# Two-layer hybrid block: the low part of a third of the feed-forward weight units from an accumulating load

## The chip, the cores and the metric

The kernel runs on one core of one Trainium2 chip. The metric is the device time of one execution in microseconds (us), the median of several runs of the same program. TensorE is written PE, its weight loads PEld, VectorE is DVE, ScalarE is ACT, GpSimd is POOL, and SP is the engine that issues most of the transfers.

## What is computed

The reference applies two layers to 256 tokens of width 1024, all in float32:

```
for i in range(DEPTH):
    x = x + 0.5 * swiglu(rmsnorm(x, ffn1_norm[i]), ffn1_w1[i], ffn1_w3[i], ffn1_w2[i])
    x = x + hybrid_mixer(rmsnorm(x, mix_norm[i]), w_in[i], ...)
    x = x + 0.5 * swiglu(rmsnorm(x, ffn2_norm[i]), ffn2_w1[i], ffn2_w3[i], ffn2_w2[i])
    gate = jax.nn.sigmoid(rmsnorm(x, ple_norm[i]) @ ple_gate[i])
    x = x + gate * (p[i] @ ple_proj[i])
return rmsnorm(x, final_norm)
```

where `swiglu(h, w1, w3, w2) = (silu(h @ w1) * (h @ w3)) @ w2` with an inner width of 2816. Each of the four feed-forward stages (two a layer) multiplies by 1024 x 5632 and then by 2816 x 1024 weights. The change touches these four stages alone.

## The kernel before

**Products in two parts.** A float32 product is made of three products of 12-bit parts (`mm3`, L280): high by high, high by low, low by high. So each weight tile is needed twice in the core's memory, as `hi` (the value rounded to the type fp32r) and as `lo` (what the rounding left).

**The stream of weights.** All weights come in units of 128 x 2048 numbers (1 MB), in the order of their use, through the class `Stream`. `issue` (L143) loads a unit into one of 3 `raw` buffers (L149, a transfer issued by SP) and splits it by halves of 1024 columns into a `hi` and a `lo` tile, of which there are 5 each:

```
nc.scalar.activation(hi[:, s:f], raw[:, a + s:a + f], AF.Copy)
nc.vector.tensor_tensor(lo[:, s:f], raw[:, a + s:a + f], hi[:, s:f].bitcast(F32), op=OP.subtract)
```

ACT makes `hi` (L158) and DVE makes `lo` (L159). `next` (L163) keeps 3 units ahead of the one that is used. A `hi` or `lo` tile can be written again when PE has read it for the last time, and a `raw` buffer can be loaded again when ACT and DVE have read it.

**The feed-forward stage** (`ffn`, L375). The first matrix is used in 11 chunks of 512 columns, two units (four halves, called h0 to h3 here, two blocks of 128 rows each) a chunk. PE goes through a chunk token tile by token tile (`rows`, L338): first all four halves for token tile 0, then all four for token tile 1. Each token tile takes 24 products of 128 x 512. So the halves of a chunk are set free one after another while token tile 1 goes by, and the halves of the next chunk are made into them just then: four halves are in use and the fifth buffer is the next chunk's h0. After each token tile ACT takes a silu (L387), DVE multiplies (L389), PE transposes the result (L277) and ACT and DVE split it (L395, L396). The second matrix is used in 11 units of 2 x 128 rows (`pairs`, L348), each unit wholly before the next; a unit takes 24 products.

**What sets the order.** A scheduler puts each engine's instructions in a fixed order when the program is built; engines run their queues in that order and wait for one another by semaphores. Semaphores of the loads that SP issues are called DMAHW in the rows of the order, those of transfers that POOL issues DMASW. POOL has no work within the feed-forward stages but the reciprocal root of the rows' squares at their end (L298, L299).

Of the kernel before, what the change touches and what calls it, by code (L numbers as in the profile page):

```python
# [13 lines left out]
AF = mybir.ActivationFunctionType  # L14
OP = mybir.AluOpType
# [16 lines left out]
# columns of the constants  # L32
# [11 lines left out]
# columns of a layer's small weights  # L44
# [53 lines left out]
def lay_out(i):  # L98
    """The arrays of the program: the inputs' own numbers in the order in which the core reads them."""
# [36 lines left out]
class Stream:  # L136
    """The weights' units in the order of their use: load, then split into two parts of 12 bits."""
# [5 lines left out]
    def issue(self, step=HALF_UNIT):  # L143
        ap, cols = self.units[self.issued]
# [6 lines left out]
        for a in range(0, cols, HALF_UNIT):  # L151
# [3 lines left out]
            hi, lo = k.tile("hi", [128, HALF_UNIT], F32R), k.tile("lo", [128, HALF_UNIT], F32R)  # L155
            for s in range(0, e, step):
                f = min(e, s + step)
                nc.scalar.activation(hi[:, s:f], raw[:, a + s:a + f], AF.Copy)  # L158
                nc.vector.tensor_tensor(lo[:, s:f], raw[:, a + s:a + f], hi[:, s:f].bitcast(F32), op=OP.subtract)  # L159
# [10 lines left out]
class Kern:  # L170
    # tiles of a tag, and their bytes of a partition
# [18 lines left out]
    # ---- tiles  # L190
# [33 lines left out]
    def constants(self):  # L224
        """What the mixers alone need."""
# [18 lines left out]
    def units(self, stages):  # L244
        a = self.a
        units = []
        for s in stages:
            if s[0] == "ffn":
                _, l, n = s
                units += [(a[f"up{n}"][l, u], UNIT) for u in range(2 * NCH)]  # L250
                units += [(a[f"dn{n}"][l, u], UNIT) for u in range(NCH)]
# [12 lines left out]
        return units  # L264

    # ---- shared pieces
    def took(self, out, passes):
        """Adds about what a product takes, in us: two of 64 rows run side by side."""
        self.pe += max(64, int(np.prod(out.shape[1:]))) * passes / (2400.0 if out.shape[0] > 64 else 4800.0)

    def mm(self, out, lhsT, rhs, start=True, stop=True, part=False):
        """lhsT^T rhs; with part, a bank holds several sums and the first product alone starts it."""
# [12 lines left out]
    def rms(self, t, h, pin=False):  # L285
        """1 / rms of the rows of x, by halves of the columns."""
# [15 lines left out]
    def parts(self, tags, n):  # L302
        """Tiles for the two parts of a feature-major activation of n k-tiles, and the getter of a k-tile's parts."""
# [3 lines left out]
    def advance(self, t, h, rms=True):  # L307
        """What the next stage needs of half the columns of a token tile of x: their transpose times the gain, in two
        parts, and 1 / rms of the rows."""
# [28 lines left out]
    def rows(self, xT, cols, tmajor, bs, kt=4):  # L338
        """x @ w for a chunk of w's columns held in units of kt k-tiles: a bank for each of the token tiles."""
# [8 lines left out]
    def pairs(self, xT, nu, tail, ready=None):  # L348
        """x @ w for w held in units of 2 k-tiles x 1024 columns; the last units are taken token tile by token tile."""
# [24 lines left out]
    # ---- stages  # L374
# [68 lines left out]
    def scaled(self, t, h):  # L443
        """1 / rms of the rows, and after the second half the output."""
# [12 lines left out]
    # ---- the mixer  # L457
    def weave(self, *streams):
        """Emits the streams' steps in about the order in which the tensor engine can take them. The first streams go
        first; a step yields how long, in us, its results take to come, or False while it waits for another stream."""  # L460
# [120 lines left out]
    def gates(self, o, z0):  # L581
        """Sigmoids of the gates and of beta, and what the decays come to."""
# [35 lines left out]
    def rope(self, z, t, nh):  # L618
        """Rotary embedding of z [128, nh, 64], the rows of a token tile."""
# [9 lines left out]
    def compress(self, g, z0, cw1):  # L629
        """The compressed keys [(kv, d), kv, n] in two parts, the compressed values [(i, kv, n), (i, kv), d] in blocks."""  # L630
# [61 lines left out]
    def silu2(self, y):  # L692
        """2 silu(y) in place of y [128, 512]."""
# [4 lines left out]
    def conv(self, g, name, z, f0):  # L698
        """z^T of 4 heads after the short convolution and twice its silu."""
# [22 lines left out]
    def products(self, name, g, t):  # L722
        """A bank with the products of a token tile's keys [j] with its keys or queries [i]."""
# [6 lines left out]
    def gdn_rows(self, g, name, t):  # L730
        """A bank with the rows of a token tile of feature-major heads."""
# [5 lines left out]
    def squares(self, ss, src):  # L737
        """Sums of the squares of [128, 4, 128] by head."""
# [350 lines left out]
```

## Time and profile before

| | |
|---|---|
| median of 3 runs | 1197.44 us (1197.08 to 1198.85) |
| profiled execution, first to last instruction (span) | 1193.4 us |
| median over that span | 4.0 us |
| PE busy | 1167.4 us (98%) |
| DVE busy | 738.0 us (62%) |
| ACT busy | 643.4 us (54%) |
| POOL busy | 98.2 us (8%) |
| transfers | 194.15 MB, mean 163 GB/s |

The profile gives the span of the profiled execution and no time of its own beside it; the runs' times are 3.7 to 5.5 us above that span, which lies ahead of the first and behind the last instruction. Busy time is the sum of an engine's instructions. A busy PE can still wait inside a stretch for as long as a matmul's recorded end covers it, so the start-to-start distance of its products is the better measure. Idle time of an engine that is not the bottleneck costs nothing.

### The profile page before, as it was taken

To read this page: it belongs to the slowest core of one execution; us is meant where nothing else is said; L and a number is where in the kernel's file an instruction comes from. 1 tells how busy PE (TensorE), PEld (TensorE's weight loads), DVE (VectorE), ACT (ScalarE), POOL (GpSimd) and SP (SyncE) were. 2 spreads that over 40 slices of the span, in tenths; PEclk is the share of its full clock that TensorE was granted. 3 is DMA by queue.
4 is the path that set the end of the run, shared out by engine and by line. 5 is a ranking of instruction groups with operands and counts; after the bars stand their busy time and mean duration, and the time that the engine had idled before them with its cause. 6 is when DMAs were issued, how large, how long until landed. Compare 5 with 4: busy or idle time off the path is not lost.

```text
span 1193.4 us, 16045 instructions
## 1 busy us (share of the span) xinstructions
PE 1167.4 (98%) x6222; PEld 934.7 (78%) x6222; DVE 738.0 (62%) x1191; ACT 643.4 (54%) x1157; POOL 98.2 (8%) x137
## 2 busy tenths in 40 slices
PE   8999999989999999999999999999899999999996
PEld 6888888877677788888878888887676778888885
DVE  5655546887846655645665564469777465565454
ACT  7544536645666554534665454375367565454463
POOL 0000000270101000000000000004500100000011
PEclk9999999999999999999999999999999999999998
DMA  8546653431213545464464575543221244555640
GB/s 314 189 164 221 237 199 125 179 108 66 86 57 141 194 163 208 171 213 154 177 212 158 195 259 199 179 178 111 102 72 71 72 164 162 203 183 201 207 176 36
DMA packets 29292, 194.15 MB, mean 163 GB/s; under 512 B 3232, under 2 KB 3616, under 8 KB 7200
## 3 DMA queue, kind: packets, MB, share of 16 engines
q1 hardware_dynamic: 28496, 191.56, 45.0%
q10 hardware_dynamic: 720, 1.57, 0.4%
q8 instruction: 49, 0.80, 0.3%
q14 instruction: 27, 0.22, 0.1%
HBM read 192.07 MB, written 1.05 MB: 162 GB/s over the span
## 4 chain that ended last, share of the span: by engine, by line
PE 91%; DVE 4%; issue 2%; ACT 1%; POOL 1%; DMA 1%; POOLq 0%; SPq 0%; ACTq 0%
PE bA L273 49%; PE bN L273 32%; PE bG L273 4%; PE bG L277 4%; PE bN L277 1%; DVE lo L159 1%; ACT hi L158 1%; DMA raw<-win 1%; POOL mn L625 0%; DMA x<-x 0%; ACT junk L925 0%; DVE y L714 0%; DVE mn L626 0%; DVE ad L786 0%; DVE g L450 0%
## 5 line engine op out<-in xcount | busy, mean ns | idle before, releaser
L273 PE MATMUL bA<-hi,xT 128*128 128x512 f32 (+1 forms) x1856 | 605.2, 398 | 1.1 <-DVE xT L327 0.5
L159 DVE TENSOR_TENSOR lo<-raw,hi 128x1024 fp32r<-128x1024 f32 (+2 forms) x358 | 437.0, 1225 | 225.2 <-ACT hi L158 204.0
L158 ACT ACTIVATE hi<-raw 128x1024 fp32r<-128x1024 f32 (+2 forms) x358 | 373.0, 1047 | 228.5 <-PE bN L273 115.8
L273 PEld LDWEIGHTS bA<-hi,xT 128*128 128x128 f32 x1856 | 345.4, 189 | 76.3 <-issue 5.9
L273 PE MATMUL bA<-lo,xT 128*128 128x512 f32 (+1 forms) x928 | 361.1, 391 | 0.0
L273 PEld LDWEIGHTS bA<-lo,xT 128*128 128x128 f32 x928 | 175.3, 189 | 32.9 <-issue 0.7
L273 PE MATMUL bN<-hi,n 128*128 128x512 f32 x480 | 155.2, 394 | 0.0
L273 PE MATMUL bN<-hi,g 128*128 128x512 f32 x448 | 139.9, 391 | 0.0
L273 PEld LDWEIGHTS bN<-hi,n 128*128 128x128 f32 x480 | 90.4, 188 | 18.4 <-issue 0.7
L273 PEld LDWEIGHTS bN<-hi,g 128*128 128x128 f32 x448 | 83.8, 188 | 17.2
L273 PE MATMUL bN<-lo,n 128*128 128x512 f32 x240 | 95.3, 397 | 0.0
L389 DVE SCALAR_TENSOR_TENSOR m<-bA,r,m 128x256 f32<-128x256 f32 x88 | 42.2, 479 | 79.7 <-ACT m L387 79.7
L273 PE MATMUL bN<-lo,g 128*128 128x512 f32 x224 | 87.8, 392 | 0.0
L387 ACT ACTIVATE m<-bA,r 128x256 f32<-128x256 f32 x88 | 41.3, 470 | 72.9 <-PE bA L273 69.7
L298 POOL TENSOR_SCALAR r<-ss 128x1 f32<-128x1 f32 x18 | 5.9, 330 | 823.0 <-ACT junk L291 823.0
L273 PEld LDWEIGHTS bN<-lo,n 128*128 128x128 f32 x240 | 45.1, 188 | 9.6 <-issue 1.1
L273 PEld LDWEIGHTS bN<-lo,g 128*128 128x128 f32 x224 | 42.1, 188 | 8.5
L327 DVE SCALAR_TENSOR_TENSOR xT<-bG,first,xT 128x128 fp32r<-128x128 f32 x96 | 31.7, 346 | 25.2 <-ACT xT L326 25.1
L326 ACT ACTIVATE xT<-bG,first 128x128 fp32r<-128x128 f32 x96 | 32.8, 361 | 16.1 <-DVE xT L327 16.0
L395 ACT ACTIVATE g<-bG 128x256 fp32r<-128x256 f32 x48 | 18.0, 374 | 42.3 <-PE bG L277 42.2
L277 PE MATMUL bG<-first,m 128*128 128x128 f32 x192 | 36.9, 273 | 2.7 <-DVE m L931 2.5
L277 PEld LDWEIGHTS bG<-first,m 128*128 128x128 f32 x192 | 25.8, 140 | 17.3 <-issue 4.5
(218 smaller groups left out, 967.8 us busy)
## 6 DMA issues: line engine op xcount, KB each, us to landing
raw<-up SPq DMA_DIRECT2D x86, 1024.0 KB, 4.9
raw<-dn SPq DMA_DIRECT2D x44, 1024.0 KB, 5.0
raw<-win SPq DMA_DIRECT2D x24, 1024.0 KB, 4.8
raw<-wout SPq DMA_DIRECT2D x8, 1024.0 KB, 4.9
raw<-gate SPq DMA_DIRECT2D x8, 1024.0 KB, 4.9
cw<-cw SPq DMA_DIRECT2D x8, 512.0 KB, 8.0
raw<-up SPq DMA_DIRECT2D x4, 512.0 KB, 7.1
raw<-proj SPq DMA_DIRECT2D x2, 1024.0 KB, 4.8
```

The source lines that it names most:

```text
L158: nc.scalar.activation(hi[:, s:f], raw[:, a + s:a + f], AF.Copy)
L159: nc.vector.tensor_tensor(lo[:, s:f], raw[:, a + s:a + f], hi[:, s:f].bitcast(F32), op=OP.subtract)
L273: self.nc.tensor.matmul(out, lhsT, rhs, start=start, stop=stop, skip_group_check=part)
L277: self.nc.tensor.transpose(out, x, self.ident[:n, :n])
L298: nc.gpsimd.tensor_scalar(r, self.ss[:, 0:1], self.ss[:, 1:2], EPS, op0=OP.add, op1=OP.add)
L326: nc.scalar.activation(hi[h][:, i, cs], b[:, i, :], AF.Copy, scale=g)
L327: nc.vector.scalar_tensor_tensor(lo[h][:, i, cs], b[:, i, :], g, hi[h][:, i, cs].bitcast(F32), op0=OP.mult, op1=OP.subtract)
L387: nc.scalar.activation(s, bs[t][:, :256], AF.Silu, scale=r[t])
L389: nc.vector.scalar_tensor_tensor(h, bs[t][:, 256:], r[t], s, op0=OP.mult, op1=OP.mult)
L395: nc.scalar.activation(hh[c // 2][o], b, AF.Copy)
```

## The change

In every feed-forward stage the units 3, 7, 11, 15 and 19 of the first matrix (the second unit, h2 and h3, of the chunks 1, 3, 5, 7 and 9) and the units 1, 3, 5, 7 and 9 of the second are marked `summed`: 10 of 33. For a half of such a unit ACT writes the negative of the rounded weights into `lo`, then `hi` as before, and POOL issues a transfer that reads the same half of the unit from the chip's memory a second time and adds it to what stands in `lo`. VectorE's subtraction of that half is gone. Units of the other stages are not summed. The lines of the changed kernel are 7 further down; the diff also takes out comments, which is left out here.

```diff
-        ap, cols = self.units[self.issued]
+        ap, cols, summed = self.units[self.issued]
...
             hi, lo = k.tile("hi", [128, HALF_UNIT], F32R), k.tile("lo", [128, HALF_UNIT], F32R)
+            if summed:
+                nc.scalar.activation(lo[:, :e], raw[:, a:a + e], AF.Copy, scale=-1.0)
+                nc.scalar.activation(hi[:, :e], raw[:, a:a + e], AF.Copy)
+                nc.gpsimd.dma_start(lo[:, :e], ap[:, a:a + e], accum_op=OP.add)
+                parts.append((hi, lo))
+                continue
             for s in range(0, e, step):
...
-                units += [(a[f"up{n}"][l, u], UNIT) for u in range(2 * NCH)]
-                units += [(a[f"dn{n}"][l, u], UNIT) for u in range(NCH)]
+                units += [(a[f"up{n}"][l, u], UNIT, u % 4 == 3) for u in range(2 * NCH)]
+                units += [(a[f"dn{n}"][l, u], UNIT, u % 2 == 1) for u in range(NCH)]
...
-        return units
+        return [u if len(u) > 2 else u + (False,) for u in units]
```

How the instructions now stand, at three places. ACT's queue before, in the first feed-forward stage, from h1 of chunk 3 to the silu of chunk 2 (`hi_316` is h1, `hi_390` and `hi_394` are h2 and h3, `hi_400` is the next chunk's h0):

```order
L158 ACTIVATE hi_316<-raw_310 128x1024 [waits PE_49]
L158 ACTIVATE hi_390<-raw_388 128x1024 [waits DMAHW6_49,PE_49]
L158 ACTIVATE hi_394<-raw_388 128x1024 [waits PE_49]
L158 ACTIVATE hi_400<-raw_398 128x1024 [waits DMAHW7_49,PE_49]
L395 ACTIVATE g_177<-bG_462 128x2x128 [waits PE_49]
```

The same place of ACT's queue now (h1 is `hi_318`, h2 is `lo_393` and `hi_392`, h3 is `lo_398` and `hi_397`, the next h0 is `hi_404`):

```order
L165 ACTIVATE hi_318<-raw_312 128x1024 [waits PE_49]
L158 ACTIVATE lo_393<-raw_390 128x1024 [waits DMAHW6_49,PE_49]
L159 ACTIVATE hi_392<-raw_390 128x1024 [waits PE_49]
L158 ACTIVATE lo_398<-raw_390 128x1024 [waits PE_49]
L159 ACTIVATE hi_397<-raw_390 128x1024 [waits PE_49]
L165 ACTIVATE hi_404<-raw_402 128x1024 [waits DMAHW7_49,PE_49]
L402 ACTIVATE g_177<-bG_466 128x2x128 [waits PE_49]
```

Two activations have come in, and h3, the next chunk's h0 and the copy of the transposed result stand behind them.

PE's queue before, where chunk 3 comes to h2 and h3 for token tile 0 (`lo_391` and `lo_395` are their low parts):

```order
L273 MATMUL bA_496<-hi_390,xT_74 128x512 [waits Activation_49]
L273 MATMUL bA_496<-lo_391,xT_74 128x512 [waits DVE_49]
L277 MATMUL bG_471<-first_64,m2_469 128x128 [waits DVE_49]
L277 MATMUL bG_471<-first_64,m2_469 128x128
L273 MATMUL bA_496<-hi_390,xT_76 128x512
L273 MATMUL bA_496<-hi_390,xT_74 128x512
L273 MATMUL bA_496<-lo_391,xT_74 128x512
L273 MATMUL bA_496<-hi_390,xT_76 128x512
L273 MATMUL bA_496<-hi_394,xT_74 128x512 [waits Activation_49]
```

And now:

```order
L280 MATMUL bA_500<-hi_392,xT_74 128x512 [waits Activation_49]
L280 MATMUL bA_500<-lo_393,xT_74 128x512 [waits DMASW2_49]
L280 MATMUL bA_500<-hi_392,xT_76 128x512
L280 MATMUL bA_500<-hi_392,xT_74 128x512
L280 MATMUL bA_500<-lo_393,xT_74 128x512
L280 MATMUL bA_500<-hi_392,xT_76 128x512
L284 MATMUL bG_475<-first_64,m2_473 128x128 [waits DVE_49]
L284 MATMUL bG_475<-first_64,m2_473 128x128
L280 MATMUL bA_500<-hi_397,xT_74 128x512 [waits Activation_49]
L280 MATMUL bA_500<-lo_398,xT_74 128x512 [waits DMASW3_49]
```

The first product with the low part of h2 and of h3 now waits for a transfer that POOL issued, and the two transposes stand four products later.

POOL's queue now, in the first feed-forward stage from h2 of chunk 3 on; before, none of these transfers was there:

```order
L160 DMA lo_393<-up1 128x1024 [waits DVE_49,Activation_49]
L160 DMA lo_398<-up1 128x1024 [waits DVE_49,Activation_49]
L160 DMA lo_571<-up1 128x1024 [waits DMASW1_49,DVE_49,Activation_49]
L160 DMA lo_576<-up1 128x1024 [waits DVE_49,Activation_49]
L160 DMA lo_749<-up1 128x1024 [waits DMASW3_49,DVE_49,Activation_49]
```

There are 80 such transfers of 512 KB in the program, 20 a feed-forward stage, and each waits for the activation that wrote the negative part.

## Rows read from the trace of the kernel before

**Rows 1.** The page, busy us (share of the span) by engine.
```profile
PE 1167.4 (98%) x6222; PEld 934.7 (78%) x6222; DVE 738.0 (62%) x1191; ACT 643.4 (54%) x1157; POOL 98.2 (8%) x137
```

**Rows 2.** Stretches of 30 us; the last three columns: PE clock, transfer share, GB/s.
```profile
core 0: us, PE busy (x) PEld busy (x) DVE busy (x) ACT busy (x) POOL busy (x), PEclk, DMA share, GB/s
90.00:120.00 30.00, 30.00 (x138) 24.51 (x137) 16.91 (x23) 14.18 (x22) 0.00 (x0) 1.00 0.60 220
...
240.00:270.00 30.00, 26.83 (x285) 21.34 (x285) 26.61 (x44) 12.38 (x19) 21.80 (x22) 0.94 0.31 111
```

**Rows 3.** Chain of waits, chunk 7 of the first feed-forward stage: start, us, what.
```profile
90.64 3.24 PE bA L273 x14
93.88 0.22 PE bG L277 x2
94.09 7.78 PE bA L273 x34
101.87 0.22 PE bG L277 x2
```

**Rows 4.** Groups by line: count, busy us, mean ns, idle before by releaser.
```profile
L159 DVE TENSOR_TENSOR lo<-raw,hi 128x1024 fp32r<-128x1024 f32 (+2 forms) x358 | 437.0, 1225 | 225.2 <-ACT hi L158 204.0
L158 ACT ACTIVATE hi<-raw 128x1024 fp32r<-128x1024 f32 (+2 forms) x358 | 373.0, 1047 | 228.5 <-PE bN L273 115.8 <-PE bA L273 109.9 <-DMA raw<-win 1.8
```

**Rows 5.** Timeline of ACT, chunk 6 to 7: start us, us, instruction, idle before.
```profile
86.37 1.06 ACT L158 ACTIVATE hi<-raw 128x1024 fp32r<-128x1024 f32 x1 [0.89 <-PE bA L273]
87.73 1.06 ACT L158 ACTIVATE hi<-raw 128x1024 fp32r<-128x1024 f32 x1 [0.30 <-PE bA L273]
89.09 1.06 ACT L158 ACTIVATE hi<-raw 128x1024 fp32r<-128x1024 f32 x1 [0.30 <-PE bA L273]
90.45 1.06 ACT L158 ACTIVATE hi<-raw 128x1024 fp32r<-128x1024 f32 x1 [0.30 <-PE bA L273]
...
91.68 0.47 ACT L387 ACTIVATE m<-bA,r 128x256 f32<-128x256 f32 x1
```

**Rows 6.** Timeline of PE, chunk 7: first low products of h2 and h3.
```profile
93.48 0.39 PE L273 MATMUL bA<-lo,xT 128*128 128x512 f32 x1
...
95.11 0.39 PE L273 MATMUL bA<-lo,xT 128*128 128x512 f32 x1
```

**Rows 7.** DMA issues: kind, count, KB each, median us from issue to landing.
```profile
raw<-up SPq DMA_DIRECT2D x86, 1024.0 KB, 4.9
...
raw<-win SPq DMA_DIRECT2D x4, 432.0 KB, 3.2
```

**Rows 8.** Timeline of SP's queue: the two loads beside chunk 7's start, merged.
```profile
88.72 3.05 SPq L149 DMA_DIRECT2D raw<-up  x2
```

**Rows 9.** One stretch over both loads' data; columns as in rows 2.
```profile
89.00:96.00 7.00, 7.00 (x34) 5.70 (x33) 4.65 (x6) 3.14 (x5) 0.00 (x0) 1.00 0.84 300
```

**Rows 10.** Timeline of DVE, chunk 7: the multiplication that its transposes wait for.
```profile
93.02 0.47 DVE L389 SCALAR_TENSOR_TENSOR m<-bA,r,m 128x256 f32<-128x256 f32 x1
```

**Rows 11.** Timeline of ACT, second matrix: second half of unit 3.
```profile
146.22 1.06 ACT L158 ACTIVATE hi<-raw 128x1024 fp32r<-128x1024 f32 x1 [3.02 <-PE bN L273]
```

**Rows 12.** Timeline of PE, second matrix: its first low products, unit 3, both halves.
```profile
153.04 0.39 PE L273 MATMUL bN<-lo,g 128*128 128x512 f32 x1
...
154.41 0.39 PE L273 MATMUL bN<-lo,g 128*128 128x512 f32 x1
```

**Rows 13.** Stretches of 1 us around a pause of PE in the mixer; columns as in rows 2.
```profile
250.00:251.00 1.00, 0.00 (x0) 0.00 (x0) 0.97 (x4) 0.97 (x1) 0.74 (x2) 1.00 0.00 0
251.00:252.00 1.00, 0.00 (x0) 0.00 (x0) 1.00 (x5) 0.09 (x1) 0.62 (x2) 1.00 0.00 0
...
253.00:254.00 1.00, 1.00 (x16) 0.89 (x12) 1.00 (x2) 0.92 (x3) 1.00 (x1) 0.89 0.06 16
254.00:255.00 1.00, 1.00 (x6) 0.35 (x7) 1.00 (x1) 0.72 (x2) 1.00 (x2) 0.50 0.00 0
...
257.00:258.00 1.00, 1.00 (x5) 0.81 (x5) 1.00 (x2) 0.00 (x0) 1.00 (x2) 0.91 0.85 360
```

## Prediction, made before the changed kernel ran

> **What bounds the kernel now.** I read the page's busy times first: PE is busy for 98% of the span, DVE for 62%, ACT for 54%, POOL for 8% [rows 1]. An average hides stages, so the stretches come next: within a feed-forward stage PE is busy 30.00 of 30 us at full clock while the transfer engines are used for 0.60 and POOL for nothing; PE's gaps lie in the mixers (26.83 of 30) [rows 2]. The chain of waits says the same more sharply: chunk 7 of the first stage is nothing but PE's products, 14, then two transposes, then 34, then two transposes, from 90.64 to 102.09, that is 11.45 us [rows 3]. DVE and ACT wait for PE there: `lo` sat idle mostly for `hi`, and `hi` for PE's release of a buffer [rows 4]. So what DVE does is not on the path, and whatever makes a `lo` tile late is.
>
> How late it may be is read from three timelines. ACT makes h1, h2 and h3 of chunk 7 at 86.37, 87.73 and 89.09, each 0.30 us after PE let go of a buffer [rows 5]. PE first multiplies by the low part of h2 at 93.48 and of h3 at 95.11 [rows 6].
>
> **The change, part by part.** *Removed:* 4 stages x 10 units x 2 halves = 80 subtractions on DVE, 80 x 1.225 = 98 us [rows 4]. They lie beside PE's products, so they are worth 0, and with PE's waits in the stages near nothing there is nothing else for them to give back.
>
> *Added on ACT:* 80 activations x 1.047 = 84 us [rows 4]. With h1 from 86.37 and each activation 1.06 us [rows 5], the negative of h2 runs from 87.50 to 88.56, its `hi` to about 89.5, the negative of h3 to 90.5, its `hi` to 91.5, the next chunk's h0 to 92.5 instead of 91.51. The silu behind them, which ended at 92.15 [rows 5], ends near 93.2, and DVE's split of that h0 ends near 93.8, with a copy and the multiplication of 0.47 us behind it; so the multiplication, which started at 93.02 [rows 10], ends near 94.7. The transposes that need it now stand behind 18 products, not 14, so near 94.8: cost 0. If that cover is gone, PE waits there for some tenths.
>
> *Moved on SP:* the loads that wait for a `raw` buffer were issued at 88.72 and about 91.4, where the merged row ends at 91.77 [rows 8]. The first still waits for DVE's h1; the second now waits for ACT's `hi` of h3, about 91.5. No change.
>
> *Added on POOL:* 80 issues. POOL has 0.00 us of other work in the stage [rows 2], so none queues behind another engine's work; the root for the next stage stands behind the last of them and is needed only when those products are over.
>
> *Added transfers, 512 KB each.* This is the term that decides. The low part of h3 can be issued when its negative is written, at 90.5, and is needed at 95.1: it may take 4.6 us; h2's, from 88.6 to 93.5, 4.9. The trace has no accumulating transfer, so I bound its price. Loads of 432 and 1024 KB land 3.2 and 4.9 us after issue [rows 7]: 1.7 us for 592 KB is 2.94 us for 1 MB, and 2.0 us fixed. The two loads of 1 MB beside this place keep the engines busy 0.84 x 7 = 5.9 us, again 2.94 each [rows 9]. So a plain copy of 512 KB costs the engines 1.47 us. An accumulation also has to fetch what stands in `lo`; I take 1.47 us as the lower and twice that, 2.94 us, as the upper price.
>
> The transfers meet exactly those two loads: the first starts at 88.72, the first accumulation at 88.6. *Lower end:* the engines serve POOL's transfers ahead, at a plain copy's price: h3 lands at 90.5 + 2.0 + 1.47 = 94.0, 1.1 us early, PE waits 0. *With the two queues served in turn*, the loads get as much as the accumulations, so h3 lands at 88.7 + 2.0 + 4 x the price: 96.6 at 1.47, 1.5 us late; 102.5 at 2.94, 7.4 us late. *Upper end:* 7.4 us. No row is nearer to one end, so I take the middle, 3.7 us; that is also what turns at one and a half copies (2.2 us) give: 99.5, 4.4 late, less a little for queues that overlap less than assumed. PE cannot win such a wait back, since it is busy in all of the rest. There are 5 such chunks in each of 4 stages: 20 x 3.7 = 74 us.
>
> The Trainium skill, "Collectives: The Full Stack", section "The bandwidth ceiling: the fold count and why AG ≠ RS ≠ AR", says that a transfer that adds runs at about half a copy's rate, because it reads two sources. It speaks against this change; by it the price is 2.94 us and the sum that of my upper end, 20 x 7.4 = 148 us. No row here can show it yet.
>
> *Second matrix.* There the fifth buffer and units used one at a time give more room. The negative of unit 3's second half is written from about 146.2 to 147.3 [rows 11] and needed at 154.41 [rows 12]: 7.1 us; the first half has more. At 2.0 + 2.94, and one load of 2.94 in turn, it takes 7.9 at most, 0.8 late; at the lower price 4.9. I take 0 and keep 0 to 16 us (20 x 0.8) for the range.
>
> *Sum:* 74 us. It is made against the profiled execution, span 1193.4 us, which ends near 1267; the median of the runs is 4.0 us above that span, so I forecast 1197.4 + 74 = **1271 us**.
>
> **The rivals.** *The transfer is hidden anyway (not slower).* If the loads get out of the way, h3 lands at 94.0 as worked out above, and nothing waits: 1197 us. It decides at a time to landing of 4.6 us. For it: the engines are used for only 0.60 of the stage [rows 2]; against it: they are used for 0.84 in just the 7 us that matter [rows 9]. The Trainium skill, "DMA: Bandwidth & Descriptors", section "Anatomy of one DMA — SWDGE (gpsimd) path", fits 2.0 us plus the bytes at 436 GB/s for a transfer from POOL, an estimate of 3.2 us for 512 KB, which sides with this rival; [rows 7] agree on the 2.0 us, on another queue.
>
> *The transfer engines become the bound.* At the double price, two units of the second matrix (2 x 24 products, about 11.0 us by the 34 products in 7.78 us of [rows 3]) need 2 x 2.94 for loads and 2 x 2.94 for accumulations, 11.8 us. Then the first matrix loses 148 us and the second some 20 x 0.8 = 16: 1197 + 164 = 1361 us. For it: an addition in place is more work than a copy; against it: nothing in the trace yet.
>
> *The clock falls.* In the mixer PE did nothing from 250 to 252, and from 253 to 258 the granted clock was 0.89, then 0.50 (1.2 instead of 2.4 GHz), then 0.91 [rows 13]; about 3.4 us at half speed, 1.7 us lost. If each of the 20 waits, at 3.7 us longer than that pause of some 2 us, did the same, 20 x 1.7 = 34 us more: 1305 us. Against it: the wait falls into two, at h2 and at h3, with products between, and dense ones right after, where the pause in the mixer was followed by small products.
>
> *Faster.* DVE's freed 98 us would have to shorten a wait of PE, and the stages have none [rows 2]; only in the passages into the mixers could a microsecond come back.
>
> That the change does not do what it says is excluded by the order: PE's products wait for POOL's transfers.
>
> **How the numbers follow.** The forecast case, PE waiting 1 to 6 us in each of the 20 chunks, gets 0.50 (its own range 1217 to 1317); hidden 0.17; engines as the bound 0.17; the clock 0.13; faster 0.03. The range 1197 to 1340 takes in the hidden case at its low end, the forecast and the clock's 1305, and leaves out the engines' 1361 and what is faster, 0.20 together. A difference under 0.2% (2.4 us) cannot be told from no change here: faster 0.03; same 0.14, most of the hidden case; slower the rest, 0.83.
>
> **What would show it.** Right: DVE's `lo` at 278 instructions and about 340 us busy, ACT about 727 us; in PE's waits a new releaser, POOL's transfer of `lo`, some 20 to 40 times, 1 to 4 us each, in the first matrix alone, at the first low products of h2 and h3; the issues listed with 5 to 9 us to landing. Wrong: no such wait (hidden); waits in the second matrix as well and transfers in use without a gap (engines as the bound); granted clock of 0.50 behind the waits (clock); or PE waiting for ACT or DVE in the chunks that have a summed unit, which would be a mistake in what I costed at 0.

## The result, and the profile after

The change makes the kernel slower by almost a fifth, and by more than the forecast's range allowed.

| | before | after |
|---|---|---|
| median of the runs | 1197.61 us (4 runs) | 1421.09 us (4 runs) |
| ratio | | 1.1881, 95% interval 1.1856 to 1.1906 |
| span of the profiled execution | 1193.4 us | 1419.2 us |
| mean granted clock of PE | 0.994 | 0.942 |

The page of the kernel after: busy time by engine (answers to [rows 1]), three groups (to [rows 4]), the two queues with their packets, MB and share of 16 engines' time, and the issues with count, size and median us to landing (to [rows 7]).

```profile
PE 1239.6 (87%) x6222; PEld 968.6 (68%) x6222; DVE 641.0 (45%) x1111; ACT 712.2 (50%) x1237; POOL 168.0 (12%) x217
...
q1 hardware_dynamic: 28496, 191.56, 38.2%
q0 software_dynamic: 11520, 41.95, 15.9%
...
L166 DVE TENSOR_TENSOR lo<-raw,hi 128x1024 fp32r<-128x1024 f32 (+2 forms) x278 | 339.2, 1225 | 378.5 <-ACT hi L165 370.3
L280 PE MATMUL bA<-lo,xT 128*128 128x512 f32 (+1 forms) x928 | 383.1, 413 | 108.4 <-DMA lo<-up 108.4
...
L158 ACT ACTIVATE lo<-raw 128x1024 fp32r<-128x1024 f32 x80 | 84.5, 1056 | 72.9 <-PE bN L280 70.2
...
raw<-up SPq DMA_DIRECT2D x86, 1024.0 KB, 5.1
raw<-dn SPq DMA_DIRECT2D x44, 1024.0 KB, 7.6
...
lo<-up POOLq DMA_DIRECT2D x40, 512.0 KB, 10.3
lo<-dn POOLq DMA_DIRECT2D x40, 512.0 KB, 8.9
```

PE has the same 6222 products, but it is idle for 1419.2 - 1239.6 = 179.6 us where it was idle for 26.0, and its products take 72.2 us more, at a lower clock. These two, 153.6 and 72.2, are the 225.8 us by which the span grew. A new releaser stands behind the idle time. The accumulations land 10.3 and 8.9 us after their issue, where SP's loads of double the size beside them land after 5.1 and 7.6. What they cost the transfer engines is read from the queues: 15.9% of 1419.2 us for 80 transfers is 2.82 us each, and 38.2% for 191.56 MB is 1.48 us per 512 KB (0.524 MB) of load. An addition costs nearly two such loads, 1.9.

The waits of PE, after (us in total, times, longest):

```profile
PE bA L280 <- DMA lo<-up: 108.4, 39, 5.9
PE bN L280 <- DMA lo<-dn: 42.4, 24, 4.0
```

So 150.8 of the 153.6 us are waits for the low parts: 5.4 us in each of the 20 summed chunks of the first matrix, 2.1 us in each of the 20 summed units of the second.

One chunk shows how it comes about. It is chunk 7 of the first stage again (answers to [rows 3, 5, 6]). ACT's timeline, with h1, then the negative and `hi` of h2, and those of h3:

```profile
112.91 1.06 ACT L165 ACTIVATE hi<-raw 128x1024 fp32r<-128x1024 f32 x1 [0.89 <-PE bA L280]
114.04 1.06 ACT L158 ACTIVATE lo<-raw 128x1024 fp32r<-128x1024 f32 x1
115.01 1.04 ACT L159 ACTIVATE hi<-raw 128x1024 fp32r<-128x1024 f32 x1
115.96 1.04 ACT L158 ACTIVATE lo<-raw 128x1024 fp32r<-128x1024 f32 x1
```

POOL's timeline, the accumulations of h2 of chunk 5, of h2 and h3 of chunk 7, and of h2 of chunk 9:

```profile
83.68 0.86 POOL L160 DMA_DIRECT2D lo<-up  x1 [27.01 <-DVE lo L166]
...
115.40 0.86 POOL L160 DMA_DIRECT2D lo<-up  x1 [28.96 <-DVE lo L166]
117.29 0.86 POOL L160 DMA_DIRECT2D lo<-up  x1 [1.03 <-ACT lo L158]
...
145.10 0.86 POOL L160 DMA_DIRECT2D lo<-up  x1 [26.94 <-DVE lo L166]
```

SP's queue, the two loads beside them (answers to [rows 8]):

```profile
115.26 3.04 SPq L150 DMA_DIRECT2D raw<-up  x2
```

The transfer queues in three stretches, 115.4 to 119.8, 119.8 to 121.8 and 121.8 to 127.9 (packets, MB, share of the engines); q0 carries the accumulations, q1 the loads:

```profile
q1 hardware_dynamic: 125, 1.02, 80.9%
...
q0 software_dynamic: 90, 0.37, 96.9%
q1 hardware_dynamic: 22, 0.05, 6.4%
...
q0 software_dynamic: 197, 0.68, 56.7%
q1 hardware_dynamic: 141, 1.02, 41.8%
```

PE's timeline, the last products before h2's low part, and the first low products of h2 and of h3:

```profile
119.57 0.61 PE L280 MATMUL bA<-hi,xT 128*128 128x512 f32 x2
124.40 0.64 PE L280 MATMUL bA<-lo,xT 128*128 128x512 f32 x1 [4.22 <-DMA lo<-up]
...
128.37 0.49 PE L280 MATMUL bA<-lo,xT 128*128 128x512 f32 x1 [0.77 <-DMA lo<-up]
```

SP's load was issued at 115.26, 0.14 us ahead of h2's accumulation, and the engines moved nearly all of it (1.02 MB) before the first packet of q0, 4.4 us after POOL's issue. Then h2 went nearly alone, and then h3 and the second load shared the engines. Two loads and two accumulations kept them busy until 127.9. At full clock PE would have wanted h2's low part at 120.0 and h3's 1.63 us later [rows 6], at 121.65; it got them at 124.40 and 128.37, so h3's is 6.7 us late.

Stretches, after (columns as in [rows 2]): one of 30 us, then some of 1 us in chunk 7 and in chunk 5, whose first low product of h3 started at 96.90.

```profile
90.00:120.00 30.00, 26.45 (x104) 20.92 (x104) 9.75 (x12) 13.14 (x18) 1.72 (x2) 0.83 0.52 164
...
125.00:126.00 1.00, 1.00 (x4) 0.81 (x3) 0.00 (x0) 0.00 (x0) 0.00 (x0) 0.50 1.00 303
128.00:129.00 1.00, 0.63 (x3) 0.54 (x4) 0.05 (x1) 0.00 (x0) 0.00 (x0) 0.99 0.00 0
...
97.00:98.00 1.00, 1.00 (x3) 0.81 (x4) 0.00 (x0) 0.00 (x0) 0.00 (x0) 0.50 0.00 0
100.00:101.00 1.00, 1.00 (x4) 0.80 (x3) 0.43 (x1) 0.00 (x0) 0.00 (x0) 0.64 0.00 0
```

After the wait for h2 the granted clock is 0.50 (1.2 GHz). In chunk 7 it is back when h3 lands, so the slow products of h2 only filled time in which PE would have waited for h3. In chunk 5 it stays low until about 100.7 (0.64 is the mean from 100 to 101), 3.8 us beyond h3's first low product, which costs 1.9 us. The distances of POOL's issues say the same: 31.7 us from chunk 5 to 7 and 29.7 from 7 to 9, where two chunks took 22.9 before [rows 3].

### The profile page after: what moved, and what is told of

Read it like the earlier page. It is cut to its first block, busy times and chain, and to the rows that moved or that the text cites. A ratio compares the mean times of both kernels' runs of the same rounds, so it can differ in the third digit from the quotient of the medians.

```text
span 1419.2 us, 16263 instructions
## 1 busy us (share of the span) xinstructions
PE 1239.6 (87%) x6222; PEld 968.6 (68%) x6222; DVE 641.0 (45%) x1111; ACT 712.2 (50%) x1237; POOL 168.0 (12%) x217
## 3 DMA queue, kind: packets, MB, share of 16 engines
q1 hardware_dynamic: 28496, 191.56, 38.2%
q0 software_dynamic: 11520, 41.95, 15.9%
## 5 line engine op out<-in xcount | busy, mean ns | idle before, releaser
L280 PE MATMUL bA<-hi,xT 128*128 128x512 f32 (+1 forms) x1856 | 637.8, 415 | 1.3 <-DVE xT L334 0.5
L166 DVE TENSOR_TENSOR lo<-raw,hi 128x1024 fp32r<-128x1024 f32 (+2 forms) x278 | 339.2, 1225 | 378.5 <-ACT hi L165 370.3
L280 PE MATMUL bA<-lo,xT 128*128 128x512 f32 (+1 forms) x928 | 383.1, 413 | 108.4 <-DMA lo<-up 108.4
L280 PEld LDWEIGHTS bA<-hi,xT 128*128 128x128 f32 x1856 | 365.5, 199 | 80.7 <-issue 5.9
L165 ACT ACTIVATE hi<-raw 128x1024 fp32r<-128x1024 f32 (+2 forms) x278 | 287.4, 1040 | 160.4 <-PE bA L280 93.9
L158 ACT ACTIVATE lo<-raw 128x1024 fp32r<-128x1024 f32 x80 | 84.5, 1056 | 72.9 <-PE bN L280 70.2
L160 POOL DMA_DIRECT2D lo<-up x40 | 35.0, 875 | 491.2 <-DVE lo L166 451.1
L396 DVE SCALAR_TENSOR_TENSOR m<-bA,r,m 128x256 f32<-128x256 f32 x88 | 42.1, 479 | 98.1 <-ACT m L394 98.1
L159 ACT ACTIVATE hi<-raw 128x1024 fp32r<-128x1024 f32 x80 | 83.4, 1043 | 0.0
L402 ACT ACTIVATE g<-bG 128x256 fp32r<-128x256 f32 x48 | 18.0, 376 | 121.8 <-PE bG L284 121.8
L160 POOL DMA_DIRECT2D lo<-dn x40 | 34.6, 865 | 315.6 <-ACT lo L158 230.6
L403 DVE TENSOR_TENSOR g<-bG,g 128x256 fp32r<-128x256 f32 x48 | 20.2, 421 | 103.7 <-ACT g L402 103.7
## 6 DMA issues: line engine op xcount, KB each, us to landing
lo<-up POOLq DMA_DIRECT2D x40, 512.0 KB, 10.3
```

The costliest lines, as they stand in the source:

```text
L158: nc.scalar.activation(lo[:, :e], raw[:, a:a + e], AF.Copy, scale=-1.0)
L159: nc.scalar.activation(hi[:, :e], raw[:, a:a + e], AF.Copy)
L160: nc.gpsimd.dma_start(lo[:, :e], ap[:, a:a + e], accum_op=OP.add)
L280: self.nc.tensor.matmul(out, lhsT, rhs, start=start, stop=stop, skip_group_check=part)
L396: nc.vector.scalar_tensor_tensor(h, bs[t][:, 256:], r[t], s, op0=OP.mult, op1=OP.mult)
L402: nc.scalar.activation(hh[c // 2][o], b, AF.Copy)
```

## The experiments

All kernels are built from the changed one. The time of the kernel before, run beside them on the same chip, was 1195.9 to 1196.7 us; losses are against that.

**Which part loses how much.** Only one of the two matrices is summed:

```diff
-                units += [(a[f"dn{n}"][l, u], UNIT, u % 2 == 1) for u in range(NCH)]
+                units += [(a[f"dn{n}"][l, u], UNIT, False) for u in range(NCH)]
```

> Only units of the first matrix are summed (40 transfers); the second matrix is as before the change. Theory A (each late transfer costs its own wait and the half clock behind it, and the two matrices don't touch each other): the 108 us of waits stay, with about 50 to 60 us of slower clock, 1345 to 1370 us, and this kernel's gain over the time before plus that of the other half alone add up to the whole 224 us. Theory B (the two disturb each other, by the clock or the transfers of one stage running into the next): the two parts alone come to less than 180 us together.

and, with the same edit on the line of `up` instead:

> Only units of the second matrix are summed (40 transfers); the first matrix is as before the change. The prediction's step, 0 us here with 0 to 16 us as its range, would give 1197 to 1213 us. Theory A (20 waits of 2.1 us at the second matrix, and a slower clock behind them): 42 us and 10 to 25 us, so 1245 to 1265 us.

The first gave 1359.4 us (ratio 1.1371, 1.1352 to 1.1389), the second 1261.5 us (1.0544, 1.0522 to 1.0567). The losses, 163.3 and 65.4 us, add up to 228.7 where both together cost 223.5, so the parts hardly touch each other. The second matrix, put at 0 in the prediction, loses 65 us. Its waits, in the run that sums it alone:

```profile
PE bN L280 <- DMA lo<-dn: 45.1, 23, 4.2
```

**ACT's work by itself.** VectorE overwrites the negative; there is no transfer:

```diff
-                nc.gpsimd.dma_start(lo[:, :e], ap[:, a:a + e], accum_op=OP.add)
+                nc.vector.tensor_tensor(lo[:, :e], raw[:, a:a + e], hi[:, :e].bitcast(F32), op=OP.subtract)
```

> ACT writes the negative into lo as in the changed kernel, 80 activations more, but no transfer adds to it: VectorE then overwrites it with the difference as before the change. The result is the same. It tests what the 84 us of ACT's work cost by themselves. Theory A (the prediction's step: they lie beside PE's products, cost 0): 1194 to 1200 us. Theory B (ACT's queue makes the copies of the transposed result or the next chunk's first half late): 1 us or more in each of 20 chunks, 1215 us or more.

1198.4 us, ratio 1.0026 (1.0015 to 1.0036), with ACT at 711.5 us. The 80 activations cost 2 to 4 us in all; 2.0 of them are two waits of PE for a multiplication (`PE bG L284 <- DVE m L396`), which the kernel before doesn't have. The rest of the loss is the transfers'.

**Adding or copying.** The same transfers without the addition:

```diff
-                nc.gpsimd.dma_start(lo[:, :e], ap[:, a:a + e], accum_op=OP.add)
+                nc.gpsimd.dma_start(lo[:, :e], ap[:, a:a + e])
```

> The 80 transfers of POOL copy the unit's half into lo instead of adding it to what stands there; everything else, the waits too, is as in the changed kernel. The low part is then the whole weight, so the computed numbers differ. Theory A (the adding itself is dear: twice the engine time of a copy, and a landing 9 to 10 us after issue): without it the queue's engine time falls from 2.82 to about 1.41 us a transfer, the landing to 5 to 6 us, PE's waits for lo in the first matrix from 108 us to 10 to 40 us, and the time from 1421 to between 1200 and 1260 us. Theory B (POOL's way of issuing is slow whatever the transfer does): landing stays at 9 to 10 us and the time at 1400 to 1421 us.

1299.8 us (ratio 1.0866, 1.085 to 1.0883): between the theories. From its page:

```profile
q0 software_dynamic: 11520, 41.95, 10.2%
...
lo<-up POOLq DMA_DIRECT2D x40, 512.0 KB, 7.1
lo<-dn POOLq DMA_DIRECT2D x40, 512.0 KB, 7.2
```

A copy costs the engines 10.2% of 1297.8 us / 80 = 1.65 us in place of 2.82, and the addition is worth 121 us. But a copy too is late, in the first matrix by 3.5 us at h3's first low product (mean of the 20 chunks): 104 us are lost without any addition.

**Earlier transfers.** Halves with a longer lead are summed: h0 of every chunk and the first half of the odd units of the second matrix; then the same without the first two chunks of a stage.

```diff
-            if summed:
+            if summed and a == 0:
...
-                units += [(a[f"up{n}"][l, u], UNIT, u % 4 == 3) for u in range(2 * NCH)]
+                units += [(a[f"up{n}"][l, u], UNIT, u % 2 == 0) for u in range(2 * NCH)]
```

> Halves with more time to come are summed instead: the first half (h0) of every chunk of the first matrix and the first half of units 1, 3, 5, 7 and 9 of the second, 64 transfers in all in place of 80; POOL adds as in the changed kernel. h0 has some 10 us between the writing of its negative and its use, the second matrix' first half about as much. Theory A (only what lands after its use costs): with a landing of 9 to 10 us waits of 0 to 1 us each, 1197 to 1240 us. Theory B (the extra traffic, ACT's extra work or the issuing costs by itself, or slows PE's clock without a wait): 64/80 of the loss or so, over 1300 us.

> As the run that sums the first halves, but without those of the first two chunks of each stage, where the lead is shortest at the start of a stage; 56 transfers, each with some 10 us between the negative and its use. Theory A (an accumulation that lands in time costs nothing, its traffic included): only the second matrix' first halves still wait now and then, some 5 us in all, 1198 to 1208 us. Theory B (the traffic or POOL's and ACT's work cost by themselves): 56/64 of that run's 18 us, 1212 us.

1213.9 us (1.0162, 1.0141 to 1.0183) with 64 transfers and 1203.7 us (1.0065, 1.005 to 1.008) with 56. A stretch of the second run inside the first matrix, and its waits for low parts:

```profile
60.00:120.00 60.00, 60.00 (x275) 48.60 (x274) 28.43 (x38) 34.57 (x49) 4.62 (x6) 1.00 0.80 236
```

```profile
PE bN L280 <- DMA lo<-dn: 4.7, 4, 1.3
PE bA L280 <- DMA lo<-up: 0.6, 1, 0.6
```

The engines are used for 0.80 there, more than in the changed kernel, and PE never stops. These transfers land 8.2 us after their issue and are wanted after 10.6. So neither the traffic nor POOL's issuing costs by itself, as far as 56 transfers show; what costs is landing after the use.

**One transfer a chunk.** Only h3 is summed (`if summed and a > 0`, second matrix not summed).

> Only the last half (h3) of each summed chunk of the first matrix is summed, 20 transfers; h2 and the second matrix are as before the change. Theory A (the transfers of h2 and h3 stand in one queue, and h3 pays for h2's): with half as many bytes in the queue h3 lands some 7 us after its issue, which is 1 us earlier than before as ACT has one activation fewer ahead of it, so PE waits 1 to 2 us in a chunk: 20 to 40 us, 0 to 20 us for the clock, 1220 to 1255 us. Theory B (each transfer costs the same on its own): half of what summing both costs, 163 / 2, or 1278 us.

1339.7 us (1.1202, 1.1165 to 1.1238), a miss for both theories: half the transfers, and 144 of the 163 us remain. They land 9.5 us after issue. h2's accumulation was not what h3 waited for; with it gone, the loads took its place on the engines.

**The loads beside them.** First those of the feed-forward units that aren't summed are left out, with additions and with copies:

> The changed kernel without the loads of the feed-forward units that aren't summed: these split the unit that was loaded last once more, so their numbers are wrong. The 80 accumulations have then next to no other transfers beside them. Theory A (they land late because the loads take turns with them on the transfer engines): landing falls to 5 to 6 us, waits in the first matrix from 108 us to under 40, time 1200 to 1270 us. Theory B (POOL's adding transfer takes 9 us by itself): landing 8 to 10 us, waits near 100 us, time over 1370 us.

> As the run without the loads of the feed-forward units that aren't summed, and with copies in place of additions too; the numbers are wrong for both reasons. By the prediction's rows (2.0 us fixed and 1.47 us of engine time) a copy of 512 KB from POOL that meets nothing lands 3.5 us after its issue, and no wait for lo is left: within 1195 to 1205 us. If instead the start of POOL's transfers takes longer than that of SP's, landing is 5 us or more and some waits stay.

1340.6 us (1.1199, 1.1179 to 1.1219) and 1259.2 us (one run). In the first, theory A missed, and theory B met the landing (9.1 us in the first matrix) but not the time, with waits of 83.3 us there. The copies landed after 6.4 us with 39.6 us of waits, as the last sentence of their expectation has it. The trace shows why: the load of the next summed unit was still issued together with each pair of accumulations, and 1 MB of it went ahead of them. A first packet 4.4 us after the issue could thus be that load or a slow start of POOL's path. A transfer of a quarter of the bytes seemed to speak for the slow start (ACT's line for the negative is cut to 256 columns too):

```diff
-                nc.gpsimd.dma_start(lo[:, :e], ap[:, a:a + e], accum_op=OP.add)
+                nc.gpsimd.dma_start(lo[:, :256], ap[:, a:a + 256], accum_op=OP.add)
+                nc.vector.tensor_tensor(lo[:, 256:e], raw[:, a + 256:a + e], hi[:, 256:e].bitcast(F32),
+                                        op=OP.subtract)
```

> The same 80 halves, but the transfer adds only 256 of the 1024 columns, and VectorE subtracts the other 768 as before the change; ACT writes the negative of those 256 alone. The bytes of a transfer are a quarter (128 KB), its start is the same. Theory A (most of the 9 to 10 us is the start of POOL's transfer, some 4.4 us from issue to the first packet, and its end): landing still 5 to 7 us, waits of some 0 to 1.5 us in a chunk, 1205 to 1250 us. Theory B (a start of 2.0 us as for the loads that SP issues, the rest is bytes): landing near 3 us, no wait, within 1195 to 1203 us.

1239.7 us (1.0362, 1.0345 to 1.0379), and 128 KB still take 6.8 us to land. The number met theory A; its reason was wrong, as the next two runs show, in which no load is left beside the transfers:

> The changed kernel without any load of a feed-forward unit but the first of each stage, those of the summed units included: all split the tile that was loaded last, so the numbers are wrong. In the run that left out the unsummed units' loads, one load of 1 MB was still issued with each pair of accumulations, and the engines served it first. Theory A (that load is what puts the first packet 4.4 us behind the issue): now it comes 1.2 to 1.7 us behind, as where no load was ahead in the changed kernel; landing 5 to 6.5 us, h3 some 1 to 2 us late, 1215 to 1245 us. Theory B (POOL's path starts slowly in the first matrix whatever the loads do): landing 8 to 9 us and some 1340 us as in that run.

> The same, with copies in place of additions; the numbers are wrong for both reasons. Theory A: landing 3.5 to 4.2 us, no wait for lo, 1194 to 1202 us. Theory B: landing 6 us, 1259 us as with one load left.

1246.5 us (1.0413, 1.0393 to 1.0434), just above theory A's range, and 1220.6 us (1.0201, 1.0186 to 1.0217). In the first, POOL issues an accumulation at 75.33 (its timeline, first fence). The queues have no packet from then to 76.8; the second fence is their row from 76.9 to 80.3, and the third the page's issues:

```profile
75.33 0.85 POOL L164 DMA_DIRECT2D lo<-up  x1 [21.99 <-DVE lo L170]
```

```profile
q0 software_dynamic: 140, 0.54, 99.2%
```

```profile
lo<-up POOLq DMA_DIRECT2D x40, 512.0 KB, 5.8
lo<-dn POOLq DMA_DIRECT2D x40, 512.0 KB, 5.7
```

POOL's path starts within about 1.6 us. The other 2.8 us of the 4.4 are the load ahead. But ahead doesn't have to mean issued first. In the run with a quarter of the bytes POOL's issue came 0.50 us before the load's, and the first packet of q0 still only after 3.2 us, with 0.39 MB of the load moved before it (third line, 97.3 to 100.5):

```profile
97.31 0.86 POOL L160 DMA_DIRECT2D lo<-up  x1 [23.32 <-ACT lo L158]
...
97.81 0.33 SPq L150 DMA_DIRECT2D raw<-up  x1
...
q1 hardware_dynamic: 47, 0.39, 55.0%
```

The copies land after 4.6 us in the first matrix; that theory A put them at 3.5 to 4.2 us, without a wait, missed by little in landing and by 19 us in time. Of the 24 us that this run loses, 9.3 are waits for low parts and 4.2 one wait for a multiplication in the first stage. Together (time in us; median landing in the first matrix):

| loads beside the transfers | adding | copying |
|---|---|---|
| all | 1421 (10.3) | 1300 (7.1) |
| one of 1 MB with each pair | 1341 (9.1) | 1259 (6.4) |
| none | 1246 (5.8) | 1221 (4.6) |

**Nothing left out: the loads wait.** The loads are made to come after the accumulations, in the kernel that sums the first matrix alone. POOL reads a column of the raw tile that the next load overwrites, once a low part has landed. With one load held, behind h2:

```diff
+        if summed:
+            held = k.tiny(1, "held")
+            nc.gpsimd.tensor_tensor(held, self.raw[:, :1], parts[0][1][:, :1].bitcast(F32), op=OP.add)
+        self.raw = raw
```

> As the run that sums the first matrix alone (1359 us), with one tiny instruction more a chunk: POOL reads one column of the raw tile of the unit ahead of the summed one together with one column of h2's low part, once that has landed. So SP's load into that raw buffer, which was issued some 0.1 us ahead of h2's accumulation, now waits until h2's low part is there. Nothing is left out. Theory A (the load that is served first makes the accumulations late): landing 5 to 8 us, waits of 1 to 2.5 us a chunk in place of 5.4, 1225 to 1275 us, if the load that now starts some 6 us later doesn't make the next chunk wait. Theory B (the start of POOL's path): within 1% of 1359 us.

1345.4 us (1.1253, 1.1234 to 1.1272), far above theory A's range and at the very edge of theory B's, 1% below 1359. By the time alone B would stand; the waits say otherwise. PE's timeline, the first low products of h2 and h3 of chunk 5:

```profile
87.00 0.50 PE L284 MATMUL bA<-lo,xT 128*128 128x512 f32 x1 [0.70 <-DMA lo<-up]
...
92.48 0.79 PE L284 MATMUL bA<-lo,xT 128*128 128x512 f32 x1 [3.59 <-DMA lo<-up]
```

Against the same chunk with no load held, the wait for h2 went from 4.1 to 0.7 us, and the one for h3 from 1.6 to 3.6: the other load, which the scheduler now put ahead in SP's queue, took turns with h3 instead. So both were held, behind h3 (`parts[1][1]`), by a second read of the unit's own raw tile:

```diff
+            nc.gpsimd.tensor_tensor(held, raw[:, :1], held, op=OP.add)
```

> As the run that sums the first matrix alone (1359 us), but now both loads that come free beside a summed chunk wait: POOL reads a column of the raw tiles of the two units together with one of h3's low part, once that has landed. In the run before, with one load held, the other went ahead of it and took turns with h3, and the waits moved from h2 (4.2 to 0.7 us) to h3 (1.0 to 3.6 us). Nothing is left out. Theory A (a load beside the accumulations makes them late): landing 5.5 to 6 us as in the run without loads, waits of 1.5 to 2 us a chunk, full clock, 1225 to 1250 us, if the two loads, which start some 5 us later, don't make the next chunk wait. Theory B (POOL's path as such, or the addition as such): over 1300 us.

1252.6 us (1.0475, 1.0458 to 1.0493), from 1359.4, just above theory A's range, with the clock at 0.995. Its waits, and ACT in the chunk behind chunk 7:

```profile
PE bA L285 <- DMA lo<-up: 32.5, 39, 2.0
PE bG L289 <- DVE m L401: 10.9, 17, 1.2
...
113.06 2.01 ACT L165 ACTIVATE hi<-raw 128x1024 fp32r<-128x1024 f32 x2 [1.23 <-DMA raw<-up]
```

At least two thirds of the first matrix' loss are the two loads. What is left is 56 us. Some 42 of them lie in the summed chunks, where h3's first low product is still 2.0 us late: the addition's own time against a lead of under 5 us. Some 16 lie in the chunks behind them and are the price of holding the loads: ACT waits for a held load there, and the multiplication that stands behind it makes PE wait, 17 times 0.6 us. No version here is faster than the kernel before.

**The clock.** Products that nobody reads fill PE's waits, then half as many:

```diff
+            if t == 0 and flags[k // kt] and k in (4, 6):
+                self.fill("N", 18 if k == 4 else 12, xT(0, t)[0], us[0](0, cols)[0])
...
+            if (t, h, k % 2) == (0, 0, 1) and flags[k // 2]:
+                self.fill("G", 9, xT(0, t)[0], u(0, 512)[0])
```

> The changed kernel with products that nobody reads put where PE waits: 18 ahead of the first products of h2 and 12 ahead of those of h3 in each summed chunk, 9 ahead of the second half of each summed unit of the second matrix; 780 products of about 0.22 us, some 170 us of work that is thrown away, in a bank that is free. Of the loss of 226 us of span, 72 us are PE's products at a slower clock. Theory A (PE's pauses make the clock fall): with the pauses filled the clock stays at 0.98 or more, the products' 72 us come back for the most part, while what the fillers take beyond the waits (170 less 151) costs up to some 20 us: 1355 to 1390 us. Theory B (the clock falls for another reason, the transfers' or ACT's activity): clock still near 0.94, and the time is 1421 us or more.

> As the run with fillers, with half as many: 9 ahead of h2's products, 6 ahead of h3's, 4 in the second matrix; 380 products in place of 780, some 87 us of work that is thrown away. Theory A (the transfers' landing sets the time, and the slow clock costs only what comes after the last landing of a chunk): waits of 50 to 90 us come back in place of the fillers, the time stays within 10 us of that run's 1412. Theory B (the full number of fillers was longer than the waits, and hid a gain of the full clock): the time falls to 1350 to 1390 us with the clock still over 0.97.

1412.5 us (1.1806, 1.1782 to 1.1831) at a mean clock of 0.991, and 1410.4 us (1.1782, 1.1759 to 1.1806) at 0.967. PE's waits in the first and in the second:

```profile
PE bN L282 <- DMA lo<-dn: 13.7, 9, 2.2
PE bA L282 <- DMA lo<-up: 9.8, 18, 2.6
```

```profile
PE bA L282 <- DMA lo<-up: 51.6, 24, 4.5
PE bN L282 <- DMA lo<-dn: 27.8, 17, 3.3
```

Filling the waits restores the clock, so the waits are what lowers it. But three kernels with clocks of 0.942, 0.967 and 0.991 end within 11 us of each other: the landing sets the time, and PE's speed while it would wait anyway does not. The first expectation (1355 to 1390) missed by taking all of the 72 us of slower products for a loss.

What the clock does cost can be read from the starts of the low products in the three traces, against the same starts in the kernel before. The first column sums the delay, over the 20 summed chunks, from the last low product of h1 to the first of h3, and, over the 20 summed units, from the last low product of the unit before to the first of the second half. The second column sums what is lost behind that, where PE waits for no transfer any more, up to the last low product of the chunk, or of the next unit:

| us, first + second matrix | up to the last late half | behind it |
|---|---|---|
| changed kernel | 140.4 + 47.4 | 22.9 + 13.3 |
| filled | 154.5 + 58.2 | -0.8 + 2.3 |
| half filled | 151.2 + 51.1 | 1.5 + 11.1 |

So the slow clock costs 36 us, half of the 72, and the fillers do give them back. They cost 25 us themselves, since the late halves' products start later by that much; whether that is only the rest of a filler when the transfer lands isn't separated here.

The Trainium skill, "TensorE: Matmul & The Clock Gate", section "HAM oscillation — how this bites in real kernels", counts as the cost of a lowered clock the time spent at it times one half. By the mean clocks (0.058 and 0.006 below full, at half speed twice as long) that is 0.058 x 1419 - 0.006 x 1193 = 75 us here. It is the 72 us of PE's rows, and twice the 36 us by which the kernel is longer for it.

## Why the prediction was right and wrong

*The bound and the direction* were right: PE had nothing to wait for, and whatever made a `lo` tile late was paid in full.

*Removed from DVE:* 97.0 us (738.0 to 641.0) against 98 forecast, worth nothing, as said.

*Added on ACT, at 0:* 2 to 4 us. The busy time came to 712.2 us, not 727, since activations that follow directly start 0.95 us apart (114.04, 115.01, 115.96), those that stood there before included, and busy time counts what overlaps once; 1.047 was counted. "If that cover is gone, PE waits there for some tenths" was seen in the run with ACT's work alone, as two waits of 1.0 us.

*SP and POOL:* both loads were issued where they had been, and nothing queued on POOL. What was overlooked is the order: the first load went 0.14 us ahead of the accumulation, not 0.1 us behind it, and was served first. By the run with a quarter of the bytes, 0.1 us behind would hardly have saved it.

*The price of an accumulation* is the step that failed: "No row is nearer to one end, so I take the middle, 3.7 us". The upper price was the true one, 2.82 us against 2.94. With it the upper end's sum held in spite of another order of service: two loads and two additions at 2.94 us each are 11.8 us of the engines, and from about 116 (80.9% of the first 4.4 us) to 127.9 they were just so long at work. It put h3 7.4 us late; 6.7 were measured in chunk 7 and 7.0 on average. 20 x 7.4 = 148 us stands against 140 measured, and 23 us for the clock make up the 163 us of the first matrix. That sum is no test of turns: with both loads and both additions to get through, the last one ends at the same time in either order. At a copy's price the order does matter; turns gave 1.5 us late there, and the run with copies measured 3.5. The fixed 2.0 us, taken from SP's loads, was too low for POOL's additions: with no load beside them they landed after 5.8 us, of which the engines' time is 19.8% of 1243.6 us / 80 = 3.08. The Trainium skill's rule of an addition at half a copy's rate ("Collectives: The Full Stack", section "The bandwidth ceiling: the fold count and why AG ≠ RS ≠ AR") comes near to this trace, 2.82 us against 1.48 for a load of SP and 1.65 for a copy of POOL. The estimate of 3.2 us from the Trainium skill's "DMA: Bandwidth & Descriptors", section "Anatomy of one DMA — SWDGE (gpsimd) path", does not agree, since even with no load beside it the addition landed after 5.7 us and the copy after 4.0 to 4.6.

*The second matrix at 0* failed too. The lead of 7.1 us was right, the landing of 7.9 at most was not: 8.9 us. In a stage's first summed unit a load goes ahead there as well, 1.03 MB before the first packet, 4.4 us after the issue; the loads themselves land after 7.6 us instead of 5.0. With no loads the waits there were 1.7 us in all. In the run that sums it alone it costs 65 us, a term with a range of 0 to 16.

*The rivals.* Hidden (1197) fell, though a longer lead makes it true (1204). The engines as the bound (1361) had the right price for the additions and was nearest, 60 us short through the second matrix and the clock. Its mechanism was not what happened: the transfers were not in use without a gap, 0.52 over 30 us; what PE waited for was a queue of some 12 us in each pair of chunks. The clock fell as that rival said, and cost 23 us in its 20 chunks, not 34, and 13 in the second matrix. Nothing became faster. Taken together, 140 us of late halves and 23 for the clock in the first matrix, 47 and 13 in the second, are 224; the runs' medians differ by 223.5. The range left out the one case, at 0.17, that came nearest.

## What to carry to other kernels

A transfer that has to land within a deadline is costed with everything that the transfer engines serve in the same microseconds, whatever is issued just before or just behind it: here 5 us of lead met 11.8 us of queued work, while such transfers with 10.6 us of lead made PE wait 0.6 us in all in the first matrix. Price an accumulation at 1.7 to 1.9 copies, as measured here, and where two ends of a price are far apart, don't take the middle without a reason; the range should then reach the far end. A lowered clock counts only for the products behind the last wait, so the busy time that it adds (72 us here) is no measure of its cost (36).

## What was not expected of the hardware

- A load of 1 MB issued 0.14 us earlier kept the other queue's first packet back until 4.4 us after its issue (1.6 us with no load there), and 0.39 MB of one issued 0.50 us later still went ahead of a smaller accumulation, and yet a load issued 0.7 us behind h3's accumulation shared the engines about equally with it, 41.8% to 56.7%. The Trainium skill, "DMA: Bandwidth & Descriptors", section "Queues, rings and completion order", says that an engine drains a whole packet from one queue and then turns to the next; the first load would agree with that if an engine's whole share of it were one such packet, while the equal turns with the second load would need smaller ones. What decides it isn't settled by these runs.
- With half of the accumulations taken away the remaining ones landed hardly earlier, 9.5 us against 10.1 with both summed: they met the loads instead of each other.
- POOL's issue of an adding transfer is recorded at 0.86 us; that of a copy at 0.53.
